# Two O/den bank pairs for the single-head units, and a new order, in the attention phase of an encoder kernel

## The chip, the cores and the metric

The kernel runs on all 8 cores of one Trainium2 chip; each core computes one of the eight sequences of the batch. The metric is the device time of the slowest core in microseconds (us). Some executions fell in a slower state: the cores of one die had a mean granted TensorE clock of 0.81 to 0.96 (0.979 to 0.997 on every core of fast runs), and the time was 1521 to 1772 us, 2 to 20% over the fastest run of the same kernel.

## The reference, cut to what matters

```python
D_MODEL, BATCH, SEQ = 1024, 8, 2048
HEAD_DIM, HEADS_PER_GROUP = 64, 5
DIL_WINDOWS, DIL_RATES = (128, 512, 2048), (1, 4, 16)       # three groups of five heads

def dilated_attention_mixer(h, w_qkv, q_norm, k_norm, w_o):
    q, k, v = ...                                           # h @ w_qkv, 15 heads
    q = rope(rms_norm(q, q_norm), pos)
    k = rope(rms_norm(k, k_norm), pos)
    for g in range(3):                                      # keys i + m*dilation, |m| <= 64
        o_g, lse_g = dilated_window_group(q[group g], k[group g], v[group g], DIL_RATES[g], radius)
    wts = softmax(lses over the three groups)               # per position and head slot
    return concat(o_g * wts[g]) @ w_o

x = x + attention(rms_norm(x));  x = x + mlp(rms_norm(x))   # layer 0
x = x + short_conv(rms_norm(x)); x = x + mlp(rms_norm(x))   # layer 1
return rms_norm(x)
```

The weighting by denominators lets the kernel add the unnormalised outputs' denominators ("den") of the three groups and divide once by the sum.

## The kernel before

The program is recorded as a list of operations with a priority each; a list scheduler with its own cost model orders them, and each engine then runs its list in order. The 15 heads make 8 "units". Units 0 to 5 hold two heads of one group, side by side in the two 64-row halves of the array ("lanes"). What is left are three single heads: unit 6 holds the fifth head of dilation 4 and the fifth of dilation 16, unit 7 the fifth of dilation 1. For each unit there is a projection (P), a QK-norm and rotary step (R), and attention: scores (S), exp, then output and denominator (O and den). When the projections have run out, only the last units' attention and the start of the output projection (W) are left for PE.

```python
UNITS = [(0, 0), (1, 0), (2, 0), (1, 1), (0, 1), (2, 1)]    # (group, pair of heads)
PMU = 4                    # from this unit on the mask is added by PE (identity matmul), not by DVE
PEB = 6                    # from this unit on rstd is broadcast by a block matmul, not through DRAM
pP, pS, pO = _Ring(range(4)), _Ring([2, 4]), (6, 7)         # P buffers; score banks; O and den bank

def attention(u, g, lanes, first, dtot):
    ncol = 128 if D == 16 else 256
    per = (512 if nl == 2 else 1024) // ncol                # key tiles of a step
    bo, bd = pO

    def out_mms(P, parts):                                  # O and den of one output block
        for q, (i, kt, oc0, pc0, nn) in enumerate(parts):
            st0, st1 = new and q == 0, fin and q == len(parts) - 1
            for kind in range(2):
                for l, (h, slot, qb, kb) in enumerate(lanes):
                    pa = P.ap[:, col + pc0:col + pc0 + nn]
                    if kind == 0:                           # V: 64 columns of the array
                        mms.append((PS(bo, oc0, oc0 + nn, rows=hs(h)), Vb[g]...[64 columns], pa, st0, st1))
                    elif nl == 2:                           # two lanes: ones, 64 columns each
                        mms.append((PS(bd, oc0, oc0 + nn, rows=hs(h)), ones1[:, 0:64], pa, st0, st1))
                    else:                                   # one lane: ones, all 128 columns
                        mms.append((PS(bd, oc0, oc0 + nn), ones1, pa, st0, st1))
        ...
        if fin:
            evacuate(B_)                                    # O to oT; den copied or added to dtot

    for s in range(16 // per):
        sb = pS.next()
        # on PE from unit PMU: two 512-column identity matmuls write the mask, then 4 to 8 score matmuls
        MMS(mms, rd, [PR(sb, nb=2)], ...)
        ACT(P.ap, psum[:, 512 * sb:512 * sb + 1024], AF.Exp, ..., scale=0.125)
        ...                                                 # O and den of the blocks that are ready

    # unit 6:  attention(6, 1, [(0, 4, q_, k_)], True, dtots[1])
    #          attention(6, 2, [(1, 4, q_, k_)], False, dtots[1])
    # unit 7:  attention(7, 0, [(0, 4, q_, k_)], False, dtots[1])
```

Of the kernel before, what the change touches and what calls it, by code (L numbers as in the profile page):

```python
# [23 lines left out]
U_END = 106416  # L24
CELL = 64

UNITS = [(0, 0), (1, 0), (2, 0), (1, 1), (0, 1), (2, 1)]

PMU = 4



FILL = 'v11 v10 p1 v20 p2 v21 p3 p4 p5 p6 p7'.split()
AHEAD = [6, 1, 6, 1, 0, 1, 3, 5]
PRI_P = [-50, 950, 1950, 2950, 3950, 4950, 5950, 6950]
PRI_R = [-150, -100, 900, 2300, 2900, 4950, 4900, 6650]
PRI_V = [0, 800, -140]
PRI_F = [6900, 7900]

PEB = 6  # L40
PS_BASE = 1 << 20


# [224 lines left out]
class _Ring:  # L268
# [4 lines left out]
    def next(self):  # L273
        b = self.ids[self.i % len(self.ids)]
        self.i += 1
        return b
# [17 lines left out]
def build_nc():  # L294
# [24 lines left out]
    with ExitStack() as st:  # L319
# [12 lines left out]
        p = Prog()  # L332
# [90 lines left out]
        dtots = [B(U_DT, 4096, True), B(U_HT + 12288, 4096, True)]  # L423
# [143 lines left out]
        def rope_a(u):  # L567

            rw, sw, rbc = raws[u % 2], sws[u], rbcs[u]
            nw = 2 if u < 7 else 1  # L570
            n = 2048 * nw
            f = nfill("sw%d" % (u // 7))
            for q in range(2):
                DMA("sp", sw.ap[q:127 + q:2, 0:n], rw.ap[1 - q:128 - q:2, 0:n], [rw.r(0, n)], [sw.r(0, n)],
                    "sw%d" % (u // 7), f, 128 * n)
            for i in range(2 * nw):
                sl = slice(i * 1024, (i + 1) * 1024)
                rr = (i * 1024, (i + 1) * 1024)
                p.op([("dve", lambda e, o=sq.ap[:, sl], i_=rw.ap[:, sl]: e.tensor_tensor(out=o, in0=i_, in1=i_, op=ALU.mult),
                       c_dve(1024, True)),  # L580
                      ("act", lambda e, o=sq.ap[:, sl], i_=rw.ap[:, sl]: e.activation(out=o, in_=i_, func=AF.Square),  # L581
                       c_act(1024, False))], None, [rw.r(*rr)], [sq.r(*rr)], None)
            if u >= PEB:
                for j in range(4 * nw):
                    b = pp.next()
                    sl, rr = slice(j * 512, (j + 1) * 512), (j * 512, (j + 1) * 512)
                    MMS([(PS(b), bd64.ap, sq.ap[:, sl], True, True)], [bd64.r(), sq.r(*rr)], [PR(b)])
                    ACT(PS(b), PS(b), AF.Ln, [PR(b), sm.r()], [PR(b)], 512, bias=eps_ap)
                    ACT(rbc.ap[:, sl], PS(b), AF.Exp, [PR(b)], [rbc.r(*rr)], 512, scale=-0.5)
                return  # L590
            b = pp.next()
            for w in range(nw):
                mms = []
                for j in range(4 * w, 4 * w + 4):
                    lo = C_SEL + 128 - 4 * j
                    mms.append((PS(b), cst.ap[:, lo:lo + 128], sq.ap[:, j * 512:(j + 1) * 512],
                                j == 0, j == 4 * nw - 1))
                MMS(mms, [CRS, sq.r(2048 * w, 2048 * w + 2048)], [PR(b)])
            rs = rst[u % 2]
            ln, lr = sq.ap[:, 0:1024].bitcast(F32), sq.r(0, 1024)  # L600
            ACT(ln, PS(b), AF.Ln, [PR(b), sm.r()], [lr], 512, bias=eps_ap)
            ACT(rs.ap, ln, AF.Exp, [lr], [rs.r()], 512, scale=-0.5, ps=False)
            dr = (2, 300000 + 1000 * (u % 2), 300000 + 1000 * (u % 2) + 64)
            DMA("sp", scr_d[u % 2].rearrange("a b -> (a b)").rearrange("(r f) -> r f", r=16), rs.ap[0:61:4, :],
                [rs.r()], [dr], "rw%d" % (u % 2), nfill("rw%d" % (u % 2)), 1 << 14)
            f = nfill("rb")
            for h in range(2):
                DMA("sp", rbc.ap[64 * h:64 * h + 64, 0:n], scr_d[u % 2, h:h + 1, 0:n].broadcast_to([64, n]),
                    [dr], [rbc.r(0, n, h)], "rb", f, 64 * 2 * n)
# [41 lines left out]
        pO = (6, 7)  # L651
# [2 lines left out]
            base = cst.ap[:, off:off + 1]  # L654
            return bass.AP(tensor=base.tensor, offset=base.offset, ap=[list(base.ap[0])] + dims)

        def attention(u, g, lanes, first, dtot):

            D = DILS[g]
            nl = len(lanes)  # L660
# [29 lines left out]
            for kt in range(16):  # L690
                for (B_, _, _, _) in contrib(kt, qsel(kt)[0]):
                    need[B_] = kt
            bo, bd = pO
            cur = [0, True]
            late = []

            def out_mms(P, parts):

                B_, new = cur
                fin = need[B_] == parts[-1][1]  # L700
                mms = []
# [4 lines that stand above are left out]
                            col = (l * 512 if nl == 2 else 0) + i * ncol  # L706
                            pa = P.ap[:, col + pc0:col + pc0 + nn]
                            if kind == 0:
                                mms.append((PS(bo, oc0, oc0 + nn, rows=hs(h)),
                                            Vb[g].ap[:, kt * 320 + slot * 64:kt * 320 + slot * 64 + 64],  # L710
                                            pa, st0, st1))
                            elif nl == 2:
                                mms.append((PS(bd, oc0, oc0 + nn, rows=hs(h)), ones1[:, 0:64], pa, st0, st1))
                            else:
                                mms.append((PS(bd, oc0, oc0 + nn), ones1, pa, st0, st1))
                wr = [PR(bo), PR(bd)] if nl == 2 else [PR(bo, lanes[0][0]), PR(bd)]
                MMS(mms, [P.r(), CR1] + [Vb[g].r(kt * 320, (kt + 1) * 320) for (_, kt, _, _, _) in parts], wr, 0.8)
                cur[1] = False
                if fin:
                    evacuate(B_)  # L720
                    cur[:] = [B_ + 1, True]

            def evacuate(B_):
                rng = (0, 2048)
# [19 lines left out]
            last = nb - 1  # L744
            on_pe = u >= PMU
            for s in range(16 // per):
# [58 lines left out]
                while late:  # L805
                    now = [x for x in late if x[0] == cur[0]]
                    if not now:
                        break
                    late = [x for x in late if x[0] != cur[0]]
                    for (_, P_, parts) in now:  # L810
                        out_mms(P_, parts)

        def finalize(units, lo, n, dtot):
            a, r_ = dtot.ap[:, lo:lo + n], dtot.r(lo, lo + n)
# [60 lines left out]
        def v_tiles(g, pri):  # L875
# [2 lines left out]
                vproj(g, kt)  # L878
            return [lambda kt=kt: one(kt) for kt in sorted(range(16), key=lambda k: k % (4 if g == 1 else 16))]

        def unit_att(u):
            p.pri = 1000 * u
            if u == PMU:

                DMA("pool", cst.ap[:, C_MB:NCST], bias_d[:, 0:NCST - C_MB], [], [CRM], "bias", 0,
                    128 * (NCST - C_MB) * 4)
                DMA("pool", ident.ap, bias_d[:, NCST - C_MB:], [], [ident.r()], "ident", 0, 1 << 16)
            q_, k_ = qk[u % 2]
            if u < 6:
                g, pr = UNITS[u]  # L890
                attention(u, g, [(0, 2 * pr, q_, k_), (1, 2 * pr + 1, q_, k_)], u % 3 == 0, dtots[0])
                if u % 3 == 2:
                    p.pri = PRI_F[u // 3]
                    for tt in range(4):
                        finalize([u - 2, u - 1, u], tt * 512, 512, dtots[0])
            elif u == 6:
                attention(6, 1, [(0, 4, q_, k_)], True, dtots[1])
                attention(6, 2, [(1, 4, q_, k_)], False, dtots[1])
            else:
                attention(7, 0, [(0, 4, q_, k_)], False, dtots[1])  # L900



# [31 lines left out]

        fill, mark = [], {0: AHEAD[0]}
        for what in FILL:
            k = int(what[1])
# [9 lines left out]
        for i in range(len(fill)):  # L948
            if i in where:
                u = where[i]  # L950
                p.pri = PRI_R[u]
                unit_rope(u)
# [208 lines left out]
def _prep_shared(inp):  # L1161
    f = lambda a: np.ascontiguousarray(np.asarray(a, dtype=np.float32))
    wqkv = f(inp["l0_w_qkv"])
    wo = f(inp["l0_w_o"])
    units = [(g, (2 * pr, 2 * pr + 1)) for g, pr in UNITS]
    heads = [[5 * g + s for s in sl] for g, sl in units] + [[9, 14], [4]]
# [37 lines left out]
def run(inputs, n_cores=8):  # L1204
    x = np.asarray(inputs["x"], dtype=np.float32)
    shared = _prep_shared(inputs)
    nc = build_nc()
    in_maps = []
    for b in range(n_cores):
        m = dict(shared)  # L1210
        m["xT"] = np.ascontiguousarray(x[b].T)
        in_maps.append(m)
    res = run_bass_kernel_spmd(nc, in_maps, core_ids=list(range(n_cores)))
    out = np.stack([np.ascontiguousarray(r["outT"].T) for r in res.results], axis=0)
    return out.astype(np.float32)
# [4 lines left out]
```

## Time and profile before

| | before |
|---|---|
| time, median of 3 runs | 1496.38 us (1495.14 to 1500.73) |
| spans of the 8 cores in the profiled run | 1490.7 to 1494.8 us |
| PE busy, core 1 | 1453.9 us (98%) |
| half-clock time between 220 and 400 us, median of the cores | 27.3 us |

The last row is the sum of the clock records with a granted clock of 0.5, core by core.

I read most of this on core 1, because its trace has every matmul record; the slowest core's (the one that the prediction quotes) lacks 136 of 7251, which makes its busy time look smaller and its idle time larger. The page of the kernel before, core 1: busy times of the engines; PE's busy tenths and granted clock in 40 slices of the span; the chain that ended last, by engine; and PE's costliest group, where the columns are busy time, mean ns of one, and idle time before it with what ended most of it.

```profile
PE 1453.9 (98%) x7251; PEld 675.2 (45%) x7251; DVE 628.9 (42%) x806; ACT 495.6 (33%) x788; POOL 526.6 (35%) x493
...
PE   4999999999999999999999999999999999999997
...
PEclk9999999799999999999999999999999999999998
...
PE 95%; DMA 2%; DVE 2%; issue 1%; POOL 0%; ACT 0%; DVEq 0%; ACTq 0%; POOLq 0%; SPq 0%
...
L354 PE MATMUL psum<-arena 128*128 128x512 bf16 (+6 forms) x7251 | 1453.9, 365 | 26.6 <-ACT arena L490 15.0
```

PE is busy nearly always, and the chain is PE. Apart from the last slice, one slice of 37 us (the eighth, from 261 us) has its clock under 0.9 of full speed. A finer view is the table by windows. Columns: window, its length, busy time of PE, weight loads, DVE, ACT and POOL with the number of instructions, the granted clock, DMA share and GB/s.

```profile
core 1: us, PE busy (x) PEld busy (x) DVE busy (x) ACT busy (x) POOL busy (x), PEclk, DMA share, GB/s
250.00:260.00 10.00, 9.39 (x73) 3.92 (x70) 6.73 (x10) 7.99 (x12) 1.49 (x2) 1.00 0.60 217
260.00:270.00 10.00, 10.00 (x56) 4.51 (x54) 6.57 (x7) 6.65 (x10) 0.75 (x1) 1.00 0.72 237
270.00:280.00 10.00, 8.35 (x29) 3.02 (x28) 7.02 (x9) 7.76 (x12) 3.24 (x5) 0.57 0.60 213
280.00:290.00 10.00, 10.00 (x37) 3.74 (x37) 5.46 (x9) 4.17 (x6) 0.56 (x1) 0.58 1.03 210
290.00:300.00 10.00, 10.00 (x54) 4.79 (x54) 3.42 (x6) 3.79 (x5) 0.75 (x1) 1.00 0.54 129
300.00:310.00 10.00, 8.00 (x40) 3.73 (x38) 6.09 (x10) 3.61 (x6) 0.88 (x1) 0.94 0.25 30
310.00:320.00 10.00, 9.19 (x27) 2.77 (x27) 6.92 (x11) 4.58 (x9) 1.32 (x2) 0.71 0.46 75
```

Between 270 and 290 us PE is busy 18.4 of 20 us at a clock of 0.57. The waits of PE on that core in the same stretch, in us in total, times and longest:

```profile
PE psum L354 <- DVE arena L370: 2.6, 4, 1.5
PE psum L354 <- DVE arena L382: 1.6, 1, 1.6
```

That is 4.2 us of waiting for evictions in 59 us. And the groups of PE's matmuls in that stretch (253 to 312 us), by shape; "128*64" means 128 rows and 64 columns of the array; the columns after the count are busy us, mean ns of one and idle before it.

```profile
L354 PE MATMUL psum<-arena 128*128 128x512 bf16 x60 | 18.0, 425 | 0.6 <-DVE arena L370 0.6
L354 PE MATMUL psum<-arena 128*64 128x256 bf16 x26 | 9.2, 354 | 1.6 <-DVE arena L382 1.6
L354 PE MATMUL psum<-arena 128*128 128x256 bf16 x26 | 8.7, 334 | 0.0
L354 PE MATMUL psum<-arena 64*128 64x256 bf16 x32 | 8.0, 389 | 0.0
```

The 26 den matmuls of 256 columns (128*128 128x256, all of units 6 and 7) are charged 8.7 us, 334 ns each. Where the matmuls of two groups alternate, each group is charged the overlap of their records: the busy times of all eleven groups of this stretch add up to 64.7 us in 59.

### The profile page before, as it was taken

How to read it: one execution, taken by the hardware profiler on the slowest of the kernel's cores; microseconds unless marked ns; L12 is line 12 of the kernel's file. 1: busy time of each engine (PE TensorE's matmuls, PEld its weight loads, DVE VectorE, ACT ScalarE, POOL GpSimd, SP SyncE). 2: the span in 40 equal slices, each digit the busy share in tenths (PEclk: the TensorE clock that was granted, in tenths of full speed). 3: DMA queues.
4: the chain of work that ended last, by engine and by line, in shares of the span. 5: the costliest groups of instructions: out<-in, count | busy, mean ns of one | idle time of the engine just before them, and what ended most of it. 6: DMA issues, size and time to landing. Idle time of an engine off the chain costs nothing.

```text
span 1494.8 us, 19962 instructions; the slowest of 8 cores (1490.7 to 1494.8 us)
## 1 busy us (share of the span) xinstructions
PE 1448.1 (97%) x7115; PEld 676.5 (45%) x7251; DVE 629.1 (42%) x806; ACT 495.9 (33%) x788; POOL 527.1 (35%) x493
## 2 busy tenths in 40 slices
PE   4999999999999999999999999999999999999996
PEld 2565444333444444444444444444444444444444
DVE  3635787559523023023039634459323032032058
ACT  3556688533310310310333433334300300301333
POOL 5200000135730630620666222256621611612552
PEclk9999999699999999999999999999999999999998
DMA  9943442810520520510410433311421312322015
GB/s 256 189 94 90 95 121 90 220 29 1 85 29 0 85 29 3 83 29 9 69 22 4 61 43 50 57 29 19 67 29 27 59 29 35 50 29 47 11 47 179
DMA packets 60848, 93.43 MB, mean 63 GB/s; under 512 B 3952, under 2 KB 41168, under 8 KB 58832
## 3 DMA queue, kind: packets, MB, share of 16 engines
q0 software_dynamic: 52416, 69.47, 27.2%
q1 hardware_dynamic: 8336, 22.68, 4.8%
q8 instruction: 60, 0.98, 0.3%
q14 instruction: 36, 0.29, 0.1%
HBM read 126.39 MB, written 8.49 MB: 90 GB/s over the span
## 4 chain that ended last, share of the span: by engine, by line
PE 92%; DVE 3%; issue 2%; DMA 2%; POOL 0%; ACT 0%; DVEq 0%; ACTq 0%; POOLq 0%
PE psum L354 92%; DVE arena L373 2%; DMA arena<-xT 2%; DVE arena L370 1%; POOL arena L386 0%; DVE arena L382 0%; ACT arena L380 0%; POOL arena L491 0%; ACT arena L490 0%; ACT arena L840 0%; DVE arena L491 0%; ACT arena L365 0%; DVE arena L476 0%; DVEq L251 0%; DVEq L319 0%
## 5 line engine op out<-in xcount | busy, mean ns | idle before, releaser
L354 PE MATMUL psum<-arena 128*128 128x512 bf16 (+6 forms) x7115 | 1448.1, 365 | 36.0 <-ACT arena L490 14.9
L354 PEld LDWEIGHTS psum<-arena 128*128 128x128 bf16 (+2 forms) x7251 | 676.5, 101 | 807.3 <-issue 116.6
L370 DVE TENSOR_TENSOR arena<-arena,psum 128x512 f32<-128x512 f32 (+1 forms) x384 | 258.2, 679 | 741.1 <-PE psum L354 726.0
L370 POOL TENSOR_TENSOR arena<-arena 128x512 bf16<-128x512 bf16 (+2 forms) x393 | 449.3, 1147 | 316.3 <-ACT arena L365 139.9
L365 ACT ACTIVATE arena<-psum 128x512 bf16<-128x512 f32 (+1 forms) x318 | 209.2, 668 | 620.0 <-PE psum L354 583.6
L373 DVE SCALAR_TENSOR_TENSOR arena<-arena 128x512 bf16<-128x512 f32 (+2 forms) x232 | 222.7, 1004 | 12.4 <-ACT arena L365 7.4
L386 POOL DMA_DIRECT2D arena<-wdn x16 | 12.6, 786 | 319.2 <-PE psum L354 319.2
L370 DVE TENSOR_TENSOR arena<-arena 128x2048 bf16<-128x2048 bf16 (+4 forms) x123 | 112.0, 959 | 27.9 <-DMA arena<-arena 12.9
L475 ACT ACTIVATE arena<-arena 128x512 f32<-128x512 f32 x111 | 69.8, 629 | 131.3 <-DVE arena L370 126.9
L380 ACT CAST arena<-psum 128x512 bf16<-128x512 f32 (+2 forms) x143 | 82.1, 578 | 89.7 <-PE psum L354 86.4
L365 ACT ACTIVATE arena<-arena 128x512 f32<-128x512 f32 (+2 forms) x83 | 54.1, 659 | 71.0 <-DVE arena L370 56.5
L382 DVE CAST arena<-psum 128x512 bf16<-128x512 f32 (+2 forms) x33 | 24.4, 739 | 48.7 <-PE psum L354 48.7
L386 POOL DMA_DIRECT2D arena<-wqk x8 | 7.4, 928 | 102.0 <-PE psum L354 102.0
L380 ACT COPY arena<-psum 128x512 f32<-128x512 f32 x38 | 23.7, 625 | 35.0 <-PE psum L354 33.9
L386 POOL DMA_DIRECT2D arena<-xT x16 | 12.1, 773 | 46.8 <-DVE arena L370 34.1
L386 POOL DMA_DIRECT2D arena<-wup x16 | 15.0, 939 | 37.4 <-PE psum L354 27.3
L365 ACT ACTIVATE arena<-psum,arena 128x512 f32<-128x512 f32 (+1 forms) x27 | 18.0, 668 | 21.9 <-PE psum L354 21.7
L581 ACT ACTIVATE arena<-arena 128x1024 bf16<-128x1024 bf16 x22 | 23.0, 1057 | 1.6
L386 POOL DMA_DIRECT2D arena<-wo x8 | 4.3, 549 | 40.3 <-PE psum L354 40.3
L491 POOL TENSOR_TENSOR arena<-arena 128x512 bf16<-128x512 f32 x8 | 11.0, 1380 | 19.0 <-DMA arena<-xT 19.0
L490 ACT ACTIVATE arena<-arena 128x512 bf16<-128x512 f32 (+1 forms) x30 | 14.2, 526 | 8.6 <-DVE arena L370 6.4
L386 POOL DMA_DIRECT2D arena<-bias x2 | 1.2, 620 | 37.8 <-DVE arena L370 37.8
(19 smaller groups left out, 57.5 us busy)
## 6 DMA issues: line engine op xcount, KB each, us to landing
arena<-xT POOLq DMA_DIRECT2D x16, 1024.0 KB, 9.2
arena<-wup POOLq DMA_DIRECT2D x16, 1024.0 KB, 10.5
arena<-wdn POOLq DMA_DIRECT2D x16, 1024.0 KB, 12.5
arena<-arena SPq DMA_DIRECT2D x14, 512.0 KB, 6.6
arena<-scr SPq DMA_DIRECT2D x12, 512.0 KB, 6.7
arena<-win POOLq DMA_DIRECT2D x8, 768.0 KB, 7.9
outT<-arena SPq DMA_DIRECT2D x24, 256.0 KB, 2.5
arena<-wqk POOLq DMA_DIRECT2D x7, 512.0 KB, 11.7
```

Source lines behind the costliest of these rows:

```text
L354: i = e.matmul(o, lhsT=l, rhs=r, start=s0, stop=s1, skip_group_check=True)
L365: return p.op("act", lambda e: e.activation(out=out, in_=in_, func=func, **kw), R, W, c_act(n, ps) + (0.09 if scale is not None and not is ...
L370: return p.op(eng, lambda e: e.tensor_tensor(out=out, in0=in0, in1=in1, op=op), R, W, cost)
L373: return p.op("dve", lambda e: e.scalar_tensor_tensor(out=out, in0=in0, scalar=scalar, in1=in1, op0=op0, op1=op1), R, W, c_dve(n, False) + ...
L380: alts.append(("act", lambda e: e.copy(out=out, in_=in_), c_act(n) + more))
L382: alts.append((e_, lambda e: e.tensor_copy(out=out, in_=in_), c_dve(n, False) + more))
L386: return p.op(eng, lambda e: e.dma_start(out=out, in_=in_), R, W, 1.3 if eng == "sp" else 1.0, chan=chan, fill=fill, nbytes=nbytes)
L475: p.op([("act", lambda e, o=o, i=xa: e.activation(out=o, in_=i, func=AF.Square), c_act(n, False)), ("dve", lambda e, o=o, i=xa: e.tensor_t ...
L490: alts = [("act", lambda e, o=o, i=xa: e.activation(out=o, in_=i, func=AF.Square), c_act(n, False)), ("dve", lambda e, o=o, i=xa: e.tensor ...
L491: ("dve", lambda e, o=o, i=xa: e.tensor_tensor(out=o, in0=i, in1=i, op=ALU.mult), c_dve(n, False))]
L581: ("act", lambda e, o=sq.ap[:, sl], i_=rw.ap[:, sl]: e.activation(out=o, in_=i_, func=AF.Square), c_act(1024, False))], None, [rw.r(*rr)], ...
```

## The change

Its intent: let unit 6's two heads take turns, each with its own O and den bank, and let unit 7 alternate between two bank pairs, so that PE computes into one pair while the other is evicted. Banks 0 and 1, which served the projections, become the second pair. The denominators of unit 6 now arrive in no fixed order, so their sum is first set to zero. Only unit 7's rstd is broadcast by product, masks move to PE a unit later, and the order and priorities of the attention phase were searched anew.

```diff
-UNITS = [(0, 0), (1, 0), (2, 0), (1, 1), (0, 1), (2, 1)]
-PMU = 4
-FILL = 'v11 v10 p1 v20 p2 v21 p3 p4 p5 p6 p7'.split()
-AHEAD = [6, 1, 6, 1, 0, 1, 3, 5]
-PRI_P, PRI_R, PRI_V, PRI_F = ...
-PEB = 6
+UNITS = [(0, 0), (1, 0), (2, 0), (2, 1), (1, 1), (0, 1)]
+PMU = 5
+FILL = 'v11 v10 p1 v20 v21 p2 p3 p4 p5 p6 p7'.split()
+AHEAD = [0, 0, 0, 1, 1, 0, 0, 4]
+PRI_P, PRI_R, PRI_V, PRI_F = ...          (other values)
+PEB = [7]
...
-        def attention(u, g, lanes, first, dtot):
+        def attention(u, g, lanes, first, dtot, rings):
...
-            bo, bd = pO
+            bo, bd = rings[0]
...
                 if fin:
                     evacuate(B_)
                     cur[:] = [B_ + 1, True]
+                    bo, bd = rings[(B_ + 1) % len(rings)]
...
                         out_mms(P_, parts)
+                yield
...
-                attention(6, 1, [(0, 4, q_, k_)], True, dtots[1])
-                attention(6, 2, [(1, 4, q_, k_)], False, dtots[1])
+                p.op("pool", lambda e, a=dtots[1].ap: e.memset(a, 0.0), [], [dtots[1].r()], 2.5)
+                run(attention(6, 1, [(0, 4, q_, k_)], False, dtots[1], [pO]),
+                    attention(6, 2, [(1, 4, q_, k_)], False, dtots[1], [(0, 1)]))
...
-                attention(7, 0, [(0, 4, q_, k_)], False, dtots[1])
+                run(attention(7, 0, [(0, 4, q_, k_)], False, dtots[1], [pO, (0, 1)]))
```

`run` advances its generators in turn, one step each.

More of the change, by code (lines that the diff above doesn't have):

```diff
@@ L25 @@
 CELL = 64
-UNITS = [(0, 0), (1, 0), (2, 0), (1, 1), (0, 1), (2, 1)]
-PMU = 4
-FILL = 'v11 v10 p1 v20 p2 v21 p3 p4 p5 p6 p7'.split()
-AHEAD = [6, 1, 6, 1, 0, 1, 3, 5]
-PRI_P = [-50, 950, 1950, 2950, 3950, 4950, 5950, 6950]
-PRI_R = [-150, -100, 900, 2300, 2900, 4950, 4900, 6650]
-PRI_V = [0, 800, -140]
-PRI_F = [6900, 7900]
-PEB = 6
+UNITS = [(0, 0), (1, 0), (2, 0), (2, 1), (1, 1), (0, 1)]
+PMU = 5
+FILL = 'v11 v10 p1 v20 v21 p2 p3 p4 p5 p6 p7'.split()
+AHEAD = [0, 0, 0, 1, 1, 0, 0, 4]
+PRI_P = [-1100, 300, 900, 3300, 4300, 4650, 6300, 6650]
+PRI_R = [-150, 300, 1300, 2300, 3300, 4300, 6300, 6300]
+PRI_V = [0, 800, 1310]
+PRI_F = [5600, 7900]
+PEB = [7]
 PS_BASE = 1 << 20
@@ L582, in rope_a @@
                        c_act(1024, False))], None, [rw.r(*rr)], [sq.r(*rr)], None)
-            if u >= PEB:
+            if u in PEB:
                 for j in range(4 * nw):
@@ L697, in out_mms @@
             def out_mms(P, parts):
+                nonlocal bo, bd
                 B_, new = cur
@@ L879, in v_tiles, with run @@
             return [lambda kt=kt: one(kt) for kt in sorted(range(16), key=lambda k: k % (4 if g == 1 else 16))]
+        def run(*steps):
+            live = list(steps)
+            while live:
+                live = [g for g in live if next(g, g) is not g]
         def unit_att(u):
@@ L890, in unit_att @@
                 g, pr = UNITS[u]
-                attention(u, g, [(0, 2 * pr, q_, k_), (1, 2 * pr + 1, q_, k_)], u % 3 == 0, dtots[0])
+                run(attention(u, g, [(0, 2 * pr, q_, k_), (1, 2 * pr + 1, q_, k_)], u % 3 == 0, dtots[0], [pO]))
                 if u % 3 == 2:
```

## The prediction

> **What bounds the kernel now.** PE: 1448 of 1495 us busy on the page; the chain of waits is 92% PE matmul. From about 323 us on it is dense (the chain shows 49 matmuls of 512 columns in 10.74 us, 219 ns each) and the change does not touch it. What matters is the stretch after the last projection (257 to 320 us), where little but units 5, 6 and 7 is left. The table by windows shows PE "busy" 28.1 of 30 us there (270 to 300), but at a granted clock of 0.62, and 16.8 of 20 us at 0.83 in 300 to 320. Core 0's clock records say 0.5 for 23.9 us from 269 us and for 6.8 us from 313 us: 15.4 us lost (12 on cores 1 and 2). The steps are multiples of 3.41 us[...]. At 219 ns per 512 columns, matmuls fill only a third of the windows before each fall. So PE starves, loses its clock, and the starved stretch grows. The timeline shows why: one O/den bank pair. In unit 7 each block is 2.28 us of PE, a DVE copy (0.68), a DVE add (0.67), then PE: 3.8 us. In unit 6 the eight evictions are longer (ACT cast 1.30, DVE copy 1.08 us). By my count 33 us of full-clock PE work (10 us of it output projection) take 60 us.
>
> **What the change does, costed.**
> 1. Unit 6's heads alternate on two bank pairs, unit 7 alternates pairs: twelve evictions of 1.4 to 2 us leave PE's path. A single-head step is 4096 columns, 1.75 us on PE against 1.04 us for its exp, so twelve steps can be PE bound at 21 us; I expect 26.[...]
> 2. Masks on PE start a unit later: 16 matmuls of 512 columns less, 3.5 us of PE; DVE gets eight 1024-wide products (0.69 each).
> 3. Unit 6's rstd through DRAM: same PE columns, but ACT loses 8 Ln and 8 Exp (0.69 + 0.61 us) and gets two: 9 us less where ACT is 90% busy (240 to 260 us). Worth 1 to 3.
> 4. Memset and four adds instead of copies: off the path.
> 5. New order: the projections end before unit 5's attention, so the tail gains unit 5's 9 to 12 us and loses most of its output-projection filler. Neutral, plus or minus 5.
>
> So the tail takes about 40 us rather than 60; with the masks, 20 to 23 us less. I take off a little for new stalls.
>
> **Prediction: 1477 us**, 1468 to 1488 in 8 of 10 cases. Faster by over 2% 0.09, within 2% 0.90, slower by over 2% 0.01.
>
> **What would show it.** Right: core 0's mean clock from 0.985 to about 0.995; no half-clock stretch over 7 us after 60 us; PE's waits for evictions at the end gone; the dense stretch starts 20 us earlier and is then as long as before within 2 us. Step 2: 16 matmuls fewer. Step 3: ACT less busy by 8 us. Wrong: half clock for over 15 us in the tail, or a gain that appears before the last projection.
>
> **What would make it wrong.** The exp-bound unit 5 without filler could itself starve PE; unit 7's last blocks hold banks 0 and 1, which the output projection wants first; the memset in POOL's queue could delay the input loads; the new order could lose PE time before the tail.

The term for the clock is cut from step 1: 12 to 15 us. The sum still contains it: the tail from 60 to 40 us, with the masks 20 to 23 us, less a little for new stalls, which gives 1477 us, 19 us under the 1496 before. The term rested on an estimate of mine that is cut with it, since no run shows it: that the clock would stay up if matmuls streamed for over half of the time. All that the kernel before had shown is that they streamed for about 0.2 to 0.4 of each 3.41 us before a fall (the tail, six cores with complete records). The estimate did not hold ("Why the prediction was wrong").

## More of the kernel before

The mean granted clock of the dies (median span and clock of four cores each):

```profile
die 0 (median of its cores): 1491.8 us, clock 0.987
die 1 (median of its cores): 1493.2 us, clock 0.986
```

Records of matmuls overlap: in the steady part of this kernel the record of a dense 512-column matmul is 379 ns long, though the next one starts 216 ns later.

What can be compared is the time from one start to the next.

## The result

| | before | after |
|---|---|---|
| time, median | 1498.21 us (4 runs) | 1493.69 us (4 runs, 1493.02 to 1494.82) |
| ratio of fast runs | | 0.9972, 95% interval 0.9948 to 0.9995 |
| spans of the cores | 1490.7 to 1494.8 us | 1488.4 to 1491.5 us |
| half-clock time, 220 to 400 us, median core | 27.3 us | 35.8 us |
| PE time of units 6 and 7 (below) | 45.7 to 47.2 us | 45.3 to 46.6 us |
| first matmul of the first MLP | 369.0 to 373.1 us | 366.5 to 370.1 us |

Ratios in this document are the mean time of one kernel's fast runs over the mean of the other's fast runs of the same rounds, so they are not quite the ratio of the medians. The change is worth 0.28%, about 4 us. I had said 1477 us, about 19 us.

The PE time of units 6 and 7 is my count from the matmul records of the cores whose records are complete (six of eight in both runs): for every score and O/den operation of these units, from its first matmul to the first matmul of whatever comes next on PE, waits included. O and den fell from 27.0 to 28.0 us before to 25.2 to 25.9 after; scores and masks rose from 18.0 to 19.2 us to 20.0 to 20.9.

The page of the changed kernel, core 1, the same lines:

```profile
PE 1458.5 (98%) x7243; PEld 676.6 (45%) x7243; DVE 630.8 (42%) x806; ACT 491.0 (33%) x778; POOL 527.1 (35%) x494
...
PE   4999999999999999999999999999999999999997
...
PEclk9999999599999999999999999999999999999998
...
PE 96%; DVE 2%; DMA 1%; issue 1%; ACT 1%; DVEq 0%; POOL 0%; ACTq 0%; POOLq 0%
...
L354 PE MATMUL psum<-arena 128*128 128x512 bf16 (+5 forms) x7243 | 1458.5, 366 | 23.3 <-ACT arena L490 15.3
```

PE's idle time before matmuls fell by 3.3 us, from 26.6 to 23.3, and its busy time rose by 4.6 us, from 1453.9 to 1458.5, though it has 8 matmuls less. The eighth slice has a lower clock than before. The windows of core 1 of the changed kernel:

```profile
250.00:260.00 10.00, 10.00 (x103) 4.28 (x101) 9.26 (x10) 9.50 (x14) 2.55 (x4) 0.97 0.73 247
260.00:270.00 10.00, 10.00 (x59) 4.82 (x57) 4.70 (x5) 4.98 (x7) 1.51 (x3) 0.88 0.95 312
270.00:280.00 10.00, 10.00 (x33) 3.40 (x32) 3.06 (x3) 3.73 (x5) 1.87 (x3) 0.50 0.55 146
280.00:290.00 10.00, 10.00 (x37) 3.83 (x36) 6.06 (x9) 6.51 (x9) 0.10 (x1) 0.50 0.98 196
290.00:300.00 10.00, 10.00 (x33) 3.42 (x33) 5.38 (x8) 2.63 (x3) 0.77 (x1) 0.50 0.31 107
300.00:310.00 10.00, 9.74 (x46) 4.34 (x46) 3.93 (x6) 4.84 (x7) 0.89 (x1) 0.91 0.00 0
310.00:320.00 10.00, 10.00 (x43) 3.88 (x42) 7.87 (x14) 4.50 (x8) 0.43 (x1) 1.00 0.72 105
```

PE is busy for every moment from 250 to 300 us, and its clock is at half from 270 to 300. The granted clock did not come back sooner; it stayed away longer (34.1 us in one stretch on this core, where before had 17.1 and 6.8). PE's waits there, and its matmul groups from 258 to 312 us:

```profile
PE psum L354 <- ACT arena L380: 0.3, 1, 0.3
```

```profile
L354 PE MATMUL psum<-arena 128*128 128x512 bf16 x41 | 15.2, 490 | 0.0
L354 PE MATMUL psum<-arena 128*64 128x256 bf16 x46 | 11.2, 332 | 0.3 <-ACT arena L380 0.3
L354 PE MATMUL psum<-arena 128*128 128x256 bf16 x26 | 9.2, 354 | 0.0
L354 PE MATMUL psum<-arena 64*128 64x256 bf16 x32 | 8.5, 407 | 0.0
```

The waits are 0.3 us where they were 4.2. The 26 den matmuls of 256 columns are still charged 9.2 us, 354 ns each; from each start to the next they take 7.1 us. There are 41 matmuls of 512 columns in this stretch where before had 60 in its own; 20 of each are masks and the rest is mostly output projection; unit 7's four rstd products come on top in before, so the changed kernel has 21 output-projection matmuls there where before had 36. And the mean clock of the dies fell a little:

```profile
die 0 (median of its cores): 1490.8 us, clock 0.984
die 1 (median of its cores): 1491.2 us, clock 0.983
```

What are these matmuls waiting for, if not for anything that the profile names? The start times of the records show it. Two groups of O and den for dilation 1 or 4, the first from core 1 of the changed kernel at full clock (from 304 us), the second from the first experiment below that removes the effect:

```
changed kernel: V and ones in turns           O matmuls first, then den (experiment e3_grouped)
start us  rows*columns  N   to the next ns    start us  rows*columns  N   to the next ns
304.395   128*64       256       229          279.539   128*64       256       128
304.624   128*128      256       213          279.667   128*64       256       109
304.837   128*64       256       229          279.776   128*64       256       109
305.066   128*128      256       213          279.885   128*64       256       205
305.279   128*64       192       203          280.090   128*128      256       120
305.482   128*128      192       187          280.210   128*128      256       109
                                              280.319   128*128      256       109
```

In these lists, where a matmul with 64 columns follows one with 128, or the other way round, the time from start to start is some 100 ns longer than where the shape stays: 213 and 229 ns from start to start instead of 109 for 256 columns at full clock. At half clock the same pairs stand 325 and 355 ns apart, against 213 without a switch. What takes the 100 ns is not shown. The records of the weight loads (95 to 106 ns long here) start 1 to 7 ns before their matmul at a switch, and some 107 ns before it, under the matmul in front, where the shape stays. So it could be a weight load that is no longer hidden; no run tests that. The kernel switches at every O and den matmul of the single-head units.

So theory 1: in units 6 and 7 PE is bound by its own matmuls and their switches. Evictions were mostly hidden behind that. Taking them away changes little, and since the array is thinly filled while PE switches, the clock is taken away all the same. Theory 2, the rival: evictions did bind, and the new order (unit 5 exposed, less filler) gave back what the banks gained.

### The profile page after: what moved, and what is told of

It is laid out like the page before. It is cut to its first block, busy times and chain, and to the rows that moved or that the text cites. A ratio compares the mean times of both kernels' runs of the same rounds, so it can differ in the third digit from the quotient of the medians.

```text
span 1491.5 us, 20081 instructions; the slowest of 8 cores (1488.4 to 1491.5 us)
## 1 busy us (share of the span) xinstructions
PE 1458.1 (98%) x7243; PEld 676.7 (45%) x7243; DVE 631.0 (42%) x806; ACT 491.2 (33%) x778; POOL 527.4 (35%) x494
## 4 chain that ended last, share of the span: by engine, by line
PE 96%; DVE 1%; issue 1%; ACT 1%; DMA 1%; POOL 0%; DVEq 0%; ACTq 0%; POOLq 0%
PE psum L354 96%; DVE arena L373 1%; DMA arena<-xT 1%; ACT arena L365 0%; DVE arena L370 0%; ACT arena L380 0%; POOL arena L386 0%; ACT arena L490 0%; ACT arena L843 0%; DVEq L319 0%; DVEq L251 0%; ACTq L251 0%; ACT arena L581 0%; ACT psum L365 0%; DVE arena L491 0%
## 5 line engine op out<-in xcount | busy, mean ns | idle before, releaser
L354 PE MATMUL psum<-arena 128*128 128x512 bf16 (+5 forms) x7243 | 1458.1, 366 | 22.4 <-ACT arena L490 14.7
L370 DVE TENSOR_TENSOR arena<-arena,psum 128x512 f32<-128x512 f32 (+1 forms) x388 | 264.4, 687 | 744.1 <-PE psum L354 740.0
L365 ACT ACTIVATE arena<-psum 128x512 bf16<-128x512 f32 (+1 forms) x310 | 205.1, 669 | 629.7 <-PE psum L354 612.1
L370 DVE TENSOR_TENSOR arena<-arena 128x2048 bf16<-128x2048 bf16 (+4 forms) x127 | 115.5, 952 | 24.1 <-ACT arena L365 14.9
L380 ACT COPY arena<-psum 128x512 f32<-128x512 f32 x35 | 20.5, 586 | 32.7 <-PE psum L354 32.6
L581 ACT ACTIVATE arena<-arena 128x1024 bf16<-128x1024 bf16 x25 | 26.3, 1058 | 2.1 <-DVE arena L382 0.7
L386 POOL DMA_DIRECT2D arena<-xT x16 | 12.0, 776 | 25.9 <-DVE arena L370 13.5
```

Of the source, the lines that this page charges most:

```text
L354: i = e.matmul(o, lhsT=l, rhs=r, start=s0, stop=s1, skip_group_check=True)
L365: return p.op("act", lambda e: e.activation(out=out, in_=in_, func=func, **kw), R, W, c_act(n, ps) + (0.09 if scale is not None and not is ...
L370: return p.op(eng, lambda e: e.tensor_tensor(out=out, in0=in0, in1=in1, op=op), R, W, cost)
L380: alts.append(("act", lambda e: e.copy(out=out, in_=in_), c_act(n) + more))
L386: return p.op(eng, lambda e: e.dma_start(out=out, in_=in_), R, W, 1.3 if eng == "sp" else 1.0, chan=chan, fill=fill, nbytes=nbytes)
L581: ("act", lambda e, o=sq.ap[:, sl], i_=rw.ap[:, sl]: e.activation(out=o, in_=i_, func=AF.Square), c_act(1024, False))], None, [rw.r(*rr)], ...
```

## The experiments

All twelve were correct. "Halves" below always means the edit of e4. The kernels of one call ran on one chip: the first four, the next four and the last four.

### e1_banks_only: the bank pairs alone

On the kernel before: `rings`, `yield`, `run`, the memset and the calls for units 6 and 7 from the diff above; `UNITS`, `PMU`, `PEB`, `FILL`, `AHEAD` and the priorities as before.

> The kernel before with the bank pairs, the turns and the memset alone; order, masks and rstd as before. Theory 1 (in units 6 and 7 PE is bound by its own matmuls: each O matmul of 64 columns is followed by a den matmul of 128 columns[...], so 256-column matmuls stand 200 to 230 ns apart and not 107; the array is too thinly filled, so the clock falls whatever the banks do): PE's time for units 6 and 7 stays at 45 us (before and after 45.8), the half-clock stretch stays at 24 us or more, time 0.2 to 0.5% under before. Theory 2 (evictions bind, bank pairs free PE, and the new order spoils it): the half-clock stretch is under 12 us and the time is 0.8 to 1.4% under before.

Measured: 1.0008 of before, interval 0.9979 to 1.0037; two of its four runs slow. The half-clock time is 41.0 us (median core), PE's time for units 6 and 7 is 46.7 to 50.9 us. With two fast runs, a gain of 0.2% or a loss of 0.4% from the banks alone can't be excluded; theory 2's gain of 0.8 to 1.4%, with under 12 us at half clock, can. The time came out above theory 1's range as well (0.2 to 0.5% under before), which I return to below.

### e2_order_only: the order, masks and rstd, without the bank pairs

```diff
-                run(attention(6, 1, [(0, 4, q_, k_)], False, dtots[1], [pO]),
-                    attention(6, 2, [(1, 4, q_, k_)], False, dtots[1], [(0, 1)]))
+                run(attention(6, 1, [(0, 4, q_, k_)], False, dtots[1], [pO]))
+                run(attention(6, 2, [(1, 4, q_, k_)], False, dtots[1], [pO]))
...
-                run(attention(7, 0, [(0, 4, q_, k_)], False, dtots[1], [pO, (0, 1)]))
+                run(attention(7, 0, [(0, 4, q_, k_)], False, dtots[1], [pO]))
```

> The changed kernel with one bank pair and unit 6's heads one after the other; order, masks and rstd as after. Theory 1: PE waits for evictions come back (idle time before matmuls up by 8 to 14 us against the 22 of after), but they cost little net, time from the same as after to 0.4% over it, so 0.997 to 1.002 of before. Theory 2 (order is the loss): slower than before, 1.003 to 1.010.

Measured: 1.0028, interval 1.0011 to 1.0045 (one of five runs slow). Half-clock time 37.5 us, units 6 and 7 take PE 46.0 to 47.2 us. PE's idle time on core 1 is 27.7 us, 4.4 more than in the changed kernel: the evictions come back as waits, but only half as much as I had expected (8 to 14 us). The order without the pairs is a little slower than before, at the edge between what the two theories had said (up to 1.002, or 1.003 and more). The run doesn't decide between them.

### e3_grouped: the same matmuls, V first, then ones

```diff
-                for q, (i, kt, oc0, pc0, nn) in enumerate(parts):
-                    st0, st1 = new and q == 0, fin and q == len(parts) - 1
-                    for kind in range(2):
+                todo = [(kind, q) for q in range(len(parts)) for kind in range(2)]
+                if nl == 1:
+                    todo.sort()
+                for kind, q in todo:
+                    (i, kt, oc0, pc0, nn) = parts[q]
+                    st0, st1 = new and q == 0, fin and q == len(parts) - 1
+                    if True:
                         for l, (h, slot, qb, kb) in enumerate(lanes):
```

The same matmuls and weight loads (7243 of each in the program), the same order of operations on PE as the changed kernel; only within an O/den operation of a single head are the matmuls sorted.

> The changed kernel with one edit: in the single-head units all O matmuls of a step come first, then all den matmuls, so that PE switches between 64-column and 128-column weights twice in a step and not at every matmul. Same instructions, same order otherwise. Theory 1: the start-to-start time of O and den matmuls of units 6 and 7 falls from 25.8 us to about 15 to 19, the half-clock stretch of 31 to 34 us gets shorter by 10 us or more, time 0.985 to 0.992 of before. Theory 2 or any theory in which waits bind: PE time falls but waits take it up, time within 0.2% of after (0.995 to 0.999).

Measured: 1479.73 us, 0.9884 of before, interval 0.9858 to 0.9910. O and den of units 6 and 7 take PE 12.8 to 14.0 us, against 25.2 to 25.9 in the changed kernel; all of units 6 and 7, 29.7 to 32.3 us against 45.3 to 46.6. The half-clock time fell from 35.8 to 3.4 us. Core 1's matmul groups of the grouped kernel, 258 to 297 us:

```profile
L354 PE MATMUL psum<-arena 128*128 128x512 bf16 x43 | 13.0, 415 | 0.7 <-ACT arena L365 0.7
L354 PE MATMUL psum<-arena 64*128 64x256 bf16 x32 | 6.8, 337 | 0.0
L354 PE MATMUL psum<-arena 128*64 128x256 bf16 x38 | 5.8, 314 | 0.3 <-ACT arena L380 0.3
L354 PE MATMUL psum<-arena 128*128 128x256 bf16 x26 | 4.6, 296 | 0.0
```

From each start to the next, the same 26 den matmuls of 256 columns now take 4.4 us where they took 7.1 us in the changed kernel. (The busy times of the lists, 4.6 and 9.2 us, overstate the drop: side by side, matmuls of one group are no longer charged their overlap. And part of the drop is the clock, which e7 below separates.) That O and den take about half the time is what theory 1 had said (15 to 19 us; it came out a little lower), and nothing that theory 2 can give: no bank, transfer or operation was changed, and the operations stand in the same order on PE in both traces.

### e4_halves: den in two halves, no switch inside O and den

```diff
                             else:
-                                mms.append((PS(bd, oc0, oc0 + nn), ones1, pa, st0, st1))
+                                for hh in (1 - h, h):
+                                    mms.append((PS(bd, oc0, oc0 + nn, rows=hs(hh)), ones1[:, 0:64], pa, st0, st1))
...
-                ... wr, 0.8)
+                ... wr, 0.8 if nl == 2 else 0.8 * 2 / 3)    # the scheduler's cost unchanged, so the same order
```

> The changed kernel with the den matmul of the single-head units done as two 64-column matmuls (one for each half of the output rows), so O and den all use 64-column weights and no switch is left within a step; there are 64+ matmuls more. Theory 1: O and den of units 6 and 7 take 12 to 16 us rather than 25.8, half clock shorter by 10 us or more, time 0.982 to 0.990 of before, a little better than the grouped one. Theory 2: within 0.2% of after. If only the number of matmuls or columns counted, it would be slower than after by some 6 us.

Measured: 1476.83 us, 0.9864 of before, interval 0.9847 to 0.9881 (one of five runs slow). O and den take PE 10.7 to 11.6 us with 54 matmuls more. An operation of eight 256-column matmuls, from its first start to the start of what follows, takes 1.68 us at full clock when V and ones alternate, 1.00 us grouped and 0.99 us as halves: twelve matmuls then, of which four pairs, on different halves of the columns, start mostly 3 to 6 ns apart. The halves save more where several operations stand in a row: the last 22 O and den matmuls of unit 7 take 4.13 us in turns, 2.79 us grouped and 1.90 us as halves (33 matmuls). The lead over grouped in the whole time is inside the intervals.

### e5_halves_on_before and e9_halves_on_before: the halves without the change

The same edit on the kernel before; nothing else.

> The kernel before with the den halves alone (no bank pairs, old order). Theory 1: the matmul switches were the limit there too, so most of the gain of the halves run (1.4% under before) comes without the bank pairs: 0.987 to 0.993; PE then waits for evictions instead, which keeps it some 5 us above the halves run on the changed kernel, and a half-clock stretch remains (10 to 25 us). If bank pairs and switches only pay together: 0.995 to 1.000.

Three of its four executions fell in the slow state. The one fast execution took 1479.7 us, and no ratio came of it, so it ran again:

> The den halves alone on the kernel before, again (three of its four executions fell in the slow state). If its one fast execution was typical: 0.987 to 0.991 of before. Then the switches were the limit before the change too, and without the change.

Measured: 0.9889, interval 0.9874 to 0.9903. The halves are worth 1.1% without the change and 1.1% with it (0.9864 over 0.9972). So the gain of the halves was there before the change was made, and the change left it as it was. Units 6 and 7 take PE 31.7 to 34.2 us.

### e6_halves_banks_before: bank pairs and halves on the old order

> The kernel before with the bank pairs and the den halves, old order, masks and rstd. Theory 1: once the switches are gone, the bank pairs are worth what I had predicted of them, so this is 0.983 to 0.990 of before, within 0.3% of the halves run on the changed kernel (0.986); the new order then is worth little. If the new order carries the gain: 0.991 or more.

Measured: 0.9914, interval 0.9899 to 0.9929. I had expected the pairs to earn what I had predicted of them as soon as the switches were gone. On the old order they do not: this is no better than the halves alone (0.9889), with more half-clock time (17.1 us against 6.8). O and den of units 6 and 7 take 15.1 to 16.7 us here and 15.6 to 16.5 in e9, so the pairs did not free PE.

### e7_fill: more dense work for PE, to keep the clock

```diff
-                    mms.append((PS(sb + q), ident.ap, map_, True, False))
+                    mms += [(PS(sb + q), ident.ap, map_, True, False)] * (3 if nl == 1 else 1)
...
-                MMS(mms, rd, [PR(sb, nb=2)], 1.0 if nl == 1 or on_pe else 0.75)
+                MMS(mms, rd, [PR(sb, nb=2)], 0.5 if nl == 1 and on_pe else 1.0 if nl == 1 or on_pe else 0.75)
```

On the changed kernel, same order on PE. Each repeated mask overwrites itself, so the result is right.

> The changed kernel where PE does each mask matmul of the single-head units three times over (the last one counts, the result is the same): 40 more dense 512-column matmuls in the stretch, 8.7 us of PE at full clock, in the same order. If the clock falls because the array is thinly filled while PE is never idle: the half-clock stretch of 31 to 34 us shrinks to under 14 us, and the time stays within 0.4% of after (0.994 to 1.001 of before) though PE has more to do. If the clock falls for another reason (waits, power, transfers): the half clock stays as long or longer and the time is 0.6 to 1.2% over after (1.003 to 1.009).

Measured: 1492.48 us, 0.9969 of before, interval 0.9954 to 0.9984: the same as the changed kernel, with 40 more matmuls of 512 columns (8.6 us at 216 ns). The half-clock time fell from 35.8 to 3.4 us. Windows of core 1 of the filled kernel, to be held against those of the changed kernel above, and the dies:

```profile
260.00:270.00 10.00, 10.00 (x61) 5.00 (x60) 3.79 (x4) 3.56 (x5) 0.55 (x1) 1.00 0.88 289
270.00:280.00 10.00, 10.00 (x39) 3.80 (x37) 1.77 (x2) 4.38 (x5) 1.52 (x3) 0.83 0.45 128
280.00:290.00 10.00, 10.00 (x56) 5.02 (x56) 7.45 (x11) 6.62 (x10) 0.98 (x2) 1.00 0.81 164
290.00:300.00 10.00, 10.00 (x52) 4.36 (x49) 6.33 (x10) 3.57 (x4) 0.77 (x1) 1.00 0.57 152
300.00:310.00 10.00, 9.74 (x50) 4.69 (x50) 5.74 (x11) 5.72 (x11) 0.89 (x1) 1.00 0.23 23
```

```profile
die 0 (median of its cores): 1489.5 us, clock 0.995
die 1 (median of its cores): 1487.3 us, clock 0.995
```

PE was busy all the time in both kernels, and the clock was at half for 35.8 us in one and 3.4 us in the other. So it is not idle time that takes the clock away here, but how much of the array works. This can be counted. All half-clock stretches in the traces between 60 and 420 us, from 3.4 to 41.0 us, are whole multiples of 3.41 us, so I took windows of that length: the columns that stream in a window (the windows laid so that the clock changes at their edges), each matmul weighted by the part of the 128*128 array that it uses, as a share of what a full array at full clock would stream. In all fourteen kernels (the cores with complete records, windows at full clock between 60 and 350 us), the clock fell after 134 windows, and 122 of those had a fill under 0.34. It stayed up after 6514 windows, of which 34 were under 0.34. The line is not sharp, but it sorts well. Columns alone sort worse: the line that lets 16 of the 6514 through (0.45) has only 86 of the 134 falls under it.

O and den of units 6 and 7 take PE 20.0 to 20.5 us in this run, at full clock and with switches; 25.2 to 25.9 at mostly half clock. So in O and den the half clock cost some 5 us, and the switches some 6 to 7 (20.0 against the 12.8 to 14.0 of the grouped run).

### e8_halves_dve_masks: no masks on PE

`PMU = 8` in the kernel of e4, so that every mask is a DVE product.

> The changed kernel with the den halves and all masks as DVE products (no mask matmuls and no bias load): 40 matmuls of 512 columns (8.6 us at full clock) and 20 switches less for PE, some 15 us more for DVE. If PE is still what binds the end: 0.978 to 0.986 of before. If the masks serve as filler that keeps the clock up, or DVE is now the limit: 0.986 to 0.995.

Measured: 0.9879, interval 0.9855 to 0.9903, in the second range. PE has 36 matmuls less than in e4 and gains nothing; the half-clock time is back at 30.7 us. That fits dense mask matmuls which paid for themselves by keeping the clock. That DVE became a limit as well is possible (PE waits 7.7 us for ACT and 5.9 us for DVE on the slowest core); the run does not tell these two apart.

### e10_halves_order, e11_halves_unit6_pairs, e12_halves_again: are the pairs worth anything?

e10 is e2 with halves. e11 is e4 with `[pO]` for unit 7 (pairs in unit 6 only). e12 is e4 again, on the same chip as the others and e9.

> Den halves on the changed kernel's order, masks and rstd, but one bank pair and unit 6's heads one after the other. If the bank pairs earn their keep only on the new order once the switches are gone: 0.989 to 0.994, clearly over the run with halves and pairs (0.986). If the pairs are worth nothing here either: within 0.2% of it.

> Den halves on the changed kernel, pairs and turns kept in unit 6, but unit 7 on one pair, so that banks 0 and 1 come free for the output projection when unit 6 ends. If unit 7's second pair costs filler (PE has output projection to do while unit 7's evictions run): 0.983 to 0.986, under the run with halves. If unit 7's evictions bind more: 0.987 to 0.990.

> The changed kernel with den halves once more, on the same chip as the three others, as their yardstick: 0.9847 to 0.9881 of before as the first time.

Measured: e10 0.9909 (0.9893 to 0.9925), e11 0.9878 (0.9860 to 0.9896), e12 0.9864 (0.9847 to 0.9882, one of four runs slow). On the new order the pairs are worth something: 0.45% between e10 and e12, whose intervals do not touch. Between 250 and 325 us PE waits 4.5 us for DVE in e10 and 2.6 in e12 (median core; on core 1 it is 5.8 and 4.8), and O and den of units 6 and 7 take 14.8 to 16.8 us in e10 and 10.7 to 11.6 in e12. Unit 7's second pair does not cost filler as I had guessed; without it e11 is a little slower, within the intervals. The dies of e12:

```profile
die 0 (median of its cores): 1473.2 us, clock 0.995
die 1 (median of its cores): 1472.7 us, clock 0.994
```

All of it in one table (ratio to before, and the half-clock time of the median core in the profiled run):

| | V and ones in turns | den in halves |
|---|---|---|
| old order, one pair | 1 (before), 27.3 us | 0.9889 (e9), 6.8 us |
| old order, two pairs | 1.0008 (e1), 41.0 us | 0.9914 (e6), 17.1 us |
| new order, one pair | 1.0028 (e2), 37.5 us | 0.9909 (e10), 11.9 us |
| new order, two pairs | 0.9972 (after), 35.8 us | 0.9864 (e12), 3.4 us |

The column step is 0.9 to 1.2% in every row. Within a row the operations stand in the same order on PE in both traces. Between the rows they don't, since the scheduler orders the list anew, so a row step is the pairs together with what the scheduler made of them. The row steps are small, and the pairs pay only together with the new order. "New order" includes the later masks and the rstd through DRAM.

e4, the changed kernel with the den in halves, is faster than both kernels: 0.9864 of before on two chips, 1.1% under the changed kernel.

## Why the prediction was wrong, point by point

**The step that failed** is step 1: "A single-head step is 4096 columns, 1.75 us on PE against 1.04 us for its exp, so twelve steps can be PE bound at 21 us; I expect 26", with the cut estimate that the clock would stay up. The term is the PE time of units 6 and 7. I predicted 26 us; it measured 45.3 to 46.6 us in the changed kernel and 45.7 to 47.2 us in the kernel before. Of these, 4.2 us before the change were waits that the banks could release (core 1); in the rest the profile shows no wait for them. Three things were missing in my sum:

- Switches. O and den cost PE 20 us at full clock rather than the 12.8 to 14.0 us of the same matmuls sorted (e7 and e3). This is the tested part.
- Strided scores. A score matmul of 256 columns starts 109 ns after the last one in dilation 1, 229 ns in dilation 4, and one of 128 columns 240 ns in dilation 16, at full clock (the first in e3 and e7, the others there and in the changed kernel). The operands of the dilated heads are read with that stride. The array's clock does not set the dilation-16 time: at half clock too, these scores stand 240 ns apart, where dense matmuls of 256 columns go from 109 to 213. Nor do the weight loads, which start at most 42 ns after the matmul in front and take at most 177 ns. No run here changes the stride, so that the stride is the cause is my reading and not shown. (Masks use 128 rows of the array and scores 64: the first score starts 311 ns after the last mask, and not 216.)
- The half clock. My estimate that it would not last rested on the first two being absent. It did not hold either: in the windows before the ten falls of the changed kernel, columns streamed for 0.33 to 0.56 of the time, mostly under half. The clock fell for longer than before, perhaps because with the waits gone the output-projection matmuls that had filled them moved behind unit 7: three output-projection operations start before unit 7's last O/den operation instead of six (counted in PE's order). That the clock follows the fill is shown by e7 (35.8 to 3.4 us at half clock); that this shift of filler is what lengthened the half clock is my reading of the order and not shown by itself.

There was also a plain miscount: dilation 16 takes eight key tiles in a single-head step, so there are ten steps and not twelve.

**The eviction waits.** I read "2.28 us of PE, a DVE copy, a DVE add, then PE" as typical of the stretch, and called 27 us of 60 starved. The table of waits had 4.2 us on core 1. The change removed just that (0.3 us left; PE's idle time over the whole run fell by 3.3 us). The rest of the 27 us stood in the profile as PE busy.

**Step 2, masks.** I said 16 matmuls fewer. It is 8 (7251 to 7243 matmuls), because the order of the pairs changed with the limit. The dilation-1 pair with 16 mask matmuls moved from unit 4 to unit 5 and stays on PE; what left PE is the dilation-16 pair, which needs only 8. And e8 shows that fewer masks on PE are not a gain where they fill the array.

**Step 3, rstd.** ACT's busy time fell by 4.6 us (495.6 to 491.0 on core 1), not by 8. Not tried alone.

**Step 4** was off the path as said, as far as the profile shows: PE has no wait on the memset. **Step 5**, "neutral, plus or minus 5": the order with one pair cost 4 us (1.0028), with two pairs the times went from 1.0008 to 0.9972 (intervals that overlap a little). It was inside the bound, but I had not seen that the pairs depend on it.

**What I said would show it wrong** did: the half clock in the tail was over 15 us. None of the four dangers that I listed shows up as the cause. That the dense part from the MLP on would be as long as before was right: 1121.7 us on core 1 before and 1121.3 us after. The chance of 0.90 for "within 2%" was right for the wrong reason.

**Theory 1 at its edges.** Its first half, switches, is shown by e3, which changes nothing else (O and den 25.2 to 25.9 us in turns, 12.8 to 14.0 sorted); its second, that thin filling and not idleness takes the clock here, by e7 (half clock 35.8 to 3.4 us). Its forecast for the pairs alone (a gain of 0.2 to 0.5%) missed.

**Still open.** On the old order the pairs left most of PE's waits for DVE in place (250 to 325 us, median core: 4.2 us before, 3.1 in e1), on the new order they took them away (4.6 in e2, none in the changed kernel). Which part of the new order does this, and why the pairs alone lengthen the half clock on the old order (41.0 us) more than the filler accounts for, was not separated. Nor was what takes the 100 ns at a switch. That the halves are better than sorting is suggested (0.9864 against 0.9884), not shown.

## What to carry to other kernels

Before giving a busy engine more buffers, take the times from one matmul's start to the next and hold them against the columns. The busy time of a group won't do, as records overlap (379 ns long, 216 ns from start to start). Here matmuls of 256 columns started 213 and 229 ns apart at full clock, twice the 109 ns without a switch, and the profile showed 4.2 us of waits in 59 us: a buffer had little to release, and the change brought 0.28%. Put matmuls that use the array in the same shape next to each other, or give them one shape; here sorting the matmuls of ten steps was worth three times the whole change (0.9884 over 0.9972). And a PE that was busy but thinly filled lost its clock here: 40 more dense matmuls took the half clock from 35.8 to 3.4 us and cost nothing (e7, 0.9969 against 0.9972 of before), and 36 fewer than in e4 brought it to 30.7 us and gained nothing (e8, 0.9879 against 0.9864).
